# Feed-forward and down stages: one pool of 8 KB places, both sums of a product ahead of their low parts

## The chip, the core and the metric

The kernel runs on one core of one Trainium2 chip. The metric is the time of one execution on the device in microseconds (us). Five engines work side by side: TensorE (PE in the profile; its weight loads are PEld), VectorE (DVE), ScalarE (ACT), GpSimd (POOL) and SyncE (SP), whose queue issues all the DMAs that matter here.

## What is computed

One decoder block on 512 tokens of 1024 channels, in float32. Only its last step, the SwiGLU feed-forward, is touched:

```python
D_FF = 2816
h2 = rmsnorm(x, g_ffn[l])
ff = (jax.nn.silu(h2 @ w_gate[l]) * (h2 @ w_up[l])) @ w_down[l]
x = x + ff
```

## The kernel before

**Arithmetic.** Each float32 operand is split into a high part (a cast to fp32r, on ScalarE) and a low part (operand minus high part, on VectorE). A product is three matmuls: high by high, low by high, high by low. `part` (L938) makes both parts of a block of weights, 128 x 1024; `split_x` (L878) those of the tokens' side.

**Gate and up, six groups.** `GROUPS` (L915) cuts the 2816 hidden channels into five groups of 512 and one of 256. In a group the gate and up weights form a 2 by 2 block matrix B11, B12, B21, B22, each block in two halves v = 0, 1. Seven products of blocks and of sums of blocks take the place of eight. `gu` (L953) issues one product: 24 matmuls of 512 columns, the first 12 with the parts of half 0, the last 12 with those of half 1. In a group after the first, the order on TensorE is: y with B21, four transposes each of two chunks (`put_h`, L1018, the group before turned for the down product), x with B11 (two more chunks are turned in its middle), z with S1, x with S2, x with S3, z with S4, x with A22. The weights of S1, S2, S3 and A22 are sums of two blocks, made in place by VectorE (`sum_of`, L949). S3 adds to the same PSUM banks as S2, and between them `keep` (L1031, copy at L1033) saves the banks with ScalarE: S3 can't write a bank before its copy is done.

**Places.** Parts rotate over three places (`ring_parts`, L930), so the cast of a part waits until TensorE is done with the part three before it. Two of the three are separate tiles for high and low part. The blocks' halves are separate tiles of 4 KB, loaded by `load_group` (L918) when the former content of each is no longer read.

**Down.** Channels 1024 to 2815 of the hidden side are multiplied one chunk of 128 at a time: `prepare(k)` (L967) loads a chunk of `w_down` and makes the parts of it and of the turned hidden chunk, and `whole` (L1105) runs 24 matmuls into eight banks. Fourteen chunks, k = 8 to 21. Between them `p_sums` (L989) makes the sums that the last stage needs.

**Last stage.** The first 1024 hidden channels use seven products again: `factors` (L1144) loads 1 MB of `w_dh` for a group of two output chunks, makes three blocks' parts (`ah`, `al`), two sums T1, T3 (`t13`, parts `ch0`, `cl0`) and T2, T4 (`t24`, parts `ch1`, `cl1`). Its pool `wd` is opened at L1125, after `wq` is released at L1124, in the same memory, so its tiles wait until all that lay there is no longer read. The order of TensorE is pinned in the order of the code; on the other engines and in SP's queue a scheduler sets it, apart from VectorE's work in the groups, which `queue` pins.

Of the kernel before, what the change touches and what calls it, by code (L numbers as in the profile page):

```python
# [14 lines left out]
ALU = mybir.AluOpType  # L15
# [38 lines left out]
def block_kernel(ctx: ExitStack, tc, x, xT, c_early, c_tab, c_late, w_qf, w_tok, w_vg, w_a, w_y, w_o, w_gu, w_gl, w_dn, w_dh, out):  # L54
# [860 lines left out]
    GROUPS = [512] * 5 + [256]  # L915
    ring, fq = [0], None

    def load_group(g, which):  # L918
        w = GROUPS[g]
        for b in which:  # L920
            if b == B21 and g % 2:
                halves_ = fq.tile([P, 2, 1024], F32, name="b21", tag="b21")
                halves_ = [halves_[:, v, :] for v in range(2)]
            else:
                halves_ = [wq.tile([P, 1024], F32, name=f"b{b}{v}", tag=f"b{b}{v}") for v in range(2)]
            for v in range(2):
                nc.sync.dma_start(out=halves_[v][:, :2 * w], in_=w_gu[g, b, v] if w == 512 else w_gl[b, v])
            raws[g][b] = [f[:, :2 * w] for f in halves_]
# [20 lines left out]
    def sum_of(g, b, c, v):  # L949
        queue(tt(out=raws[g][b][v], in0=raws[g][b][v], in1=raws[g][c][v], op=ALU.add))  # L950
# [15 lines left out]

    def prepare(k):  # L967
        n = k - HALF
        raw = wq.tile([P, 1024], F32, name="raw", tag=("b00", "b01", "b30", "b31")[n % 4])
        nc.sync.dma_start(out=raw, in_=w_dn[n])  # L970
        h, l = ring_parts()
        cast = nc.scalar.copy(out=h, in_=raw)
        if n > 0:
            after(cast, prepare.last)
        tt(out=l, in0=raw, in1=f32(h), op=ALU.subtract)
        if n % 4 == 0:
            hl = xp.tile([P, 2, S], F32R, name="hl", tag="s4")
        elif n % 4 == 3:
            hl = fq.tile([P, 2, S], F32R, name="hl", tag="b21")
        else:  # L980
            hl = wq.tile([P, 2, S], F32R, name="hl", tag=f"b2{n % 4 - 1}")
# [4 lines left out]
        tt(out=pl, in0=pf[:, k, :], in1=f32(ph), op=ALU.subtract)  # L986
        parts_of[k] = (h, l, ph, pl)

    def p_sums(j):  # L989

        fx = wq.tile([P, 4, HT], F32, name="fx", tag="b1%d" % (j % 2))
        a11, a21, a12, a22 = (pf[:, 2 * j + m2, s2 * HT:s2 * HT + HT] for m2 in range(2) for s2 in range(2))
        tt(out=fx[:, 0, :], in0=a21, in1=a22, op=ALU.subtract)
# [32 lines left out]
    for g, w in enumerate(GROUPS):  # L1026
# [17 lines left out]
        else:  # L1044
# [14 lines left out]
        parts = [part(sum_of(g, B11, B22, v)) for v in range(2)]  # L1059
        gu(x_, parts, S2, False, w)  # L1060
        keep(1, x_)
        if g == 0:
# [1 line left out]
        for tp in range(2):  # L1064
            queue(tt(out=us[tp][:, 0, :], in0=y_[tp][:, :w], in1=us[tp][:, 0, :], op=ALU.add))  # L1065
            act(out=us[tp][:, 0, :], in_=us[tp][:, 0, :], func=AF.Silu, scale=rstd2[:, tp:tp + 1])
        parts = [part(sum_of(g, B12, B22, v)) for v in range(2)]
        if g + 1 < len(GROUPS):
            load_group(g + 1, (B12,))
        gu(x_, parts, S3, False, w)  # L1070
# [2 lines left out]
        if g + 1 < len(GROUPS):  # L1073
            load_group(g + 1, (B22,))
        gu(z_, parts, S4, False, w)
        parts = [part(sum_of(g, B11, B21, v)) for v in range(2)]
        if g + 1 < len(GROUPS):
            load_group(g + 1, (B11,))
        for tp in range(2):
# [50 lines left out]
    def wtile(tag):  # L1130

        n, dt, *other = WT[tag]
        i = seen.get(tag, 0)
        seen[tag] = i + 1
        if other and i % 2:
            return fq.tile([P, n, 512], dt, name=tag, tag=other[0])
        return wd.tile([P, n, 512], dt, name=tag, tag=tag)

    def split_to(src, tags):
        h, l = wtile(tags[0]), wtile(tags[1])  # L1140
        split_to.last = nc.scalar.copy(out=h, in_=src), tt(out=l, in0=src, in1=f32(h), op=ALU.subtract)
        return h, l

    def factors(src, behind=None):  # L1144

        raw, t13, t24 = wtile("raw"), wtile("t13"), wtile("t24")
        nc.sync.dma_start(out=raw, in_=src)
# [3 lines left out]
        factors.cast, c0 = split_to.last[0], split_to(t13, ("ch0", "cl0"))  # L1151
# [5 lines left out]
        c1 = split_to(t24, ("ch1", "cl1"))  # L1157
# [79 lines left out]
    pinned[0] = False  # L1237
    fp.release()
    fq.release()
    wd.release()  # L1240
    xp.release()
    ps.release()
    drp.release()
# [104 lines left out]
```

## Time and profile before

| | us |
|---|---|
| median of 3 runs (729.04 to 730.38) | 730.36 |
| the profiled execution itself | 730.06 |
| its span, first to last instruction | 728.3 |
| TensorE busy (97%) | 707.4 |
| TensorE weight loads (81%) | 587.7 |
| VectorE busy (71%) | 520.0 |
| ScalarE busy (51%) | 373.0 |

In the slices of the page TensorE is busy nine tenths or more nearly everywhere; the exception that stands out is the third slice from the end, with 5 tenths and a granted clock of 7 tenths, and that is where the last stage begins. The mean granted clock of TensorE is 0.990. The groups of 512 take some 41.6 us each and stand between 385 and 570 us, the narrow group ends near 595 us, the down stage near 673 us.

### The profile page before, as it was taken

The numbers are of one execution on the slowest core, as the hardware profiler recorded it, in microseconds if no ns is written. First come the engines' busy times: TensorE is split into PE (matmuls) and PEld (weight loads), VectorE is DVE, ScalarE is ACT, GpSimd is POOL, SyncE is SP. The second block draws the span as 40 slices with busy tenths as digits, with TensorE's granted clock in tenths as the row PEclk, the third lists the DMA queues.
The fourth block names the chain that finished last, engine by engine and source line by source line (L and its number), as shares of the span: only waits on it lengthen the run. The fifth ranks groups of instructions, "written<-read, shape, count | busy, mean of one in ns | idle before, by whom it ended". The sixth has DMA issues, their size and how long they took to land.

```text
span 728.3 us, 9535 instructions
## 1 busy us (share of the span) xinstructions
PE 707.4 (97%) x3599; PEld 587.7 (81%) x3599; DVE 520.0 (71%) x845; ACT 373.0 (51%) x570; POOL 72.2 (10%) x90
## 2 busy tenths in 40 slices
PE   9999999999999999999998999999999989999598
PEld 6888988888877778888886878778787978888598
DVE  6798587754877757569787878687777789334584
ACT  6677363234765583236555564655555575321251
POOL 0005940202222110002210000000000000000000
PEclk9999999999999999999999999999999999999799
DMA  8900312323433212268105124060602045210412
GB/s 284 408 6 30 118 58 89 94 85 117 126 102 93 81 50 97 89 200 317 42 17 180 52 82 151 26 206 0 198 6 59 28 156 189 90 30 1 147 64 78
DMA packets 24141, 77.29 MB, mean 106 GB/s; under 512 B 2840, under 2 KB 3480, under 8 KB 23584
## 3 DMA queue, kind: packets, MB, share of 16 engines
q1 hardware_dynamic: 23952, 76.67, 32.0%
q8 instruction: 28, 0.46, 0.3%
q14 instruction: 17, 0.14, 0.1%
q10 hardware_dynamic: 144, 0.02, 0.0%
HBM read 73.52 MB, written 2.11 MB: 104 GB/s over the span
## 4 chain that ended last, share of the span: by engine, by line
PE 80%; DVE 9%; ACT 6%; issue 3%; DMA 2%; POOL 1%; ACTq 0%; SPq 0%; DVEq 0%; POOLq 0%
PE acc L72 57%; PE sc L72 15%; PE tp L72 5%; PE tp L75 3%; ACT ph L941 3%; DVE b L950 2%; DVE pl L942 2%; DVE us L1065 1%; ACT hl L941 1%; DMA raw<-in_w_dh_dram 1%; ACT us L1033 1%; DMA raw<-in_w_tok_dram 0%; POOL cb L680 0%; DMA cb<-cd 0%; DVE tq L667 0%
## 5 line engine op out<-in xcount | busy, mean ns | idle before, releaser
L154 ACT CAST wh<-raw 128x1024 fp32r<-128x1024 f32 (+1 forms) x44 | 46.1, 1049 | 84.8 <-PE acc L72 80.7
L942 DVE TENSOR_TENSOR pl<-b,ph 128x1024 fp32r<-128x1024 f32 (+1 forms) x56 | 63.3, 1138 | 36.2 <-ACT ph L941 36.2
L72 PE MATMUL acc<-ph,xfh 128*128 128x512 f32 (+1 forms) x196 | 74.3, 379 | 2.3 <-ACT us L1033 1.3
L72 PE MATMUL acc<-pl,xfh 128*128 128x512 f32 (+1 forms) x196 | 73.7, 376 | 1.1 <-DVE pl L942 0.9
L941 ACT CAST ph<-b 128x1024 fp32r<-128x1024 f32 (+1 forms) x56 | 54.8, 983 | 38.1 <-DVE b L950 27.8
L72 PE MATMUL acc<-ph,xfl 128*128 128x512 f32 (+1 forms) x196 | 72.9, 372 | 0.0
L155 DVE TENSOR_TENSOR wl<-raw,wh 128x1024 fp32r<-128x1024 f32 (+1 forms) x44 | 56.9, 1296 | 17.3 <-ACT wh L154 17.2
L72 PE MATMUL acc<-hl,xfh 128*128 128x512 f32 (+1 forms) x184 | 59.7, 384 | 3.1 <-ACT hl L941 2.3
L950 DVE TENSOR_TENSOR b<-b,b 128x1024 f32<-128x1024 f32 (+1 forms) x48 | 54.2, 1130 | 0.1
L72 PE MATMUL acc<-xh,wh 128*128 128x512 f32 x128 | 53.2, 416 | 0.0
L72 PE MATMUL acc<-wh,xh 128*128 128x512 f32 (+2 forms) x144 | 50.4, 350 | 0.0
L72 PE MATMUL acc<-xh,wl 128*128 128x512 f32 x128 | 50.1, 392 | 0.0
L72 PE MATMUL acc<-xl,wh 128*128 128x512 f32 x128 | 50.0, 391 | 0.0
L72 PE MATMUL acc<-wh,xl 128*128 128x512 f32 (+2 forms) x144 | 49.4, 343 | 0.0
L72 PE MATMUL acc<-wl,xh 128*128 128x512 f32 (+2 forms) x144 | 49.3, 342 | 0.0
L72 PEld LDWEIGHTS acc<-ph,xfh 128*128 128x128 f32 x196 | 36.9, 188 | 10.4 <-ACT us L1033 3.2
L72 PEld LDWEIGHTS acc<-pl,xfh 128*128 128x128 f32 x196 | 36.9, 188 | 10.0 <-DVE pl L942 3.7
L72 PEld LDWEIGHTS acc<-hl,xfh 128*128 128x128 f32 x184 | 34.2, 192 | 12.3 <-DVE hl L942 2.8
L942 DVE TENSOR_TENSOR hl<-b,hl 128x1024 fp32r<-128x1024 f32 (+1 forms) x28 | 31.6, 1128 | 16.5 <-ACT hl L941 16.5
L72 PEld LDWEIGHTS acc<-ph,xfl 128*128 128x128 f32 x196 | 36.9, 188 | 6.1
L941 ACT CAST hl<-b 128x1024 fp32r<-128x1024 f32 (+1 forms) x28 | 27.3, 976 | 20.8 <-DVE b L950 9.8
L72 PE MATMUL acc<-hl,xfl 128*128 128x512 f32 (+1 forms) x92 | 34.6, 376 | 0.0
(329 smaller groups left out, 1762.7 us busy)
## 6 DMA issues: line engine op xcount, KB each, us to landing
b<-in_w_gu_dram SPq DMA_DIRECT2D x40, 512.0 KB, 4.8
raw<-in_w_a_dram SPq DMA_DIRECT2D x16, 512.0 KB, 3.6
raw<-in_w_dn_dram SPq DMA_DIRECT2D x14, 512.0 KB, 3.9
blk<-in_w_vg_dram SPq DMA_DIRECT2D x8, 512.0 KB, 10.1
raw<-in_w_tok_dram SPq DMA_DIRECT2D x8, 512.0 KB, 3.5
raw<-in_w_y_dram SPq DMA_DIRECT2D x8, 512.0 KB, 3.6
raw<-in_w_o_dram SPq DMA_DIRECT2D x8, 512.0 KB, 3.6
raw<-in_w_dh_dram SPq DMA_DIRECT2D x4, 1024.0 KB, 4.8
```

What stands on the lines that cost most here:

```text
L72: in_order(nc.tensor.matmul(o, **kw))
L75: in_order(nc.tensor.transpose(out=o, in_=src, identity=ident))
L154: split_raw.last = (nc.scalar.copy(out=h[:, :width], in_=raw[:, :width]), tt(out=l[:, :width], in0=raw[:, :width], in1=f32(h)[:, :width], ...
L155: tt(out=l[:, :width], in0=raw[:, :width], in1=f32(h)[:, :width], op=ALU.subtract))
L941: nc.scalar.copy(out=h, in_=raw)
L942: low = tt(out=l, in0=raw, in1=f32(h), op=ALU.subtract)
L950: queue(tt(out=raws[g][b][v], in0=raws[g][b][v], in1=raws[g][c][v], op=ALU.add))
L1033: nc.scalar.copy(out=us[tp][:, slot, :], in_=os[tp][:, :w])
L1065: queue(tt(out=us[tp][:, 0, :], in0=y_[tp][:, :w], in1=us[tp][:, 0, :], op=ALU.add))
```

## The change

Blocks, parts and the last stage's tiles become tiles of 8 KB that hold a pair: both halves of a block (tags `b0` to `b3`, and `b2f` for B21 of odd groups), high and low part of one ring place (`r0`, `r1`, `r2`), two raw chunks of `w_down`. The pool `wd` is gone: the last stage takes places of `wq` and `fq` by name. A place is free again when both of its halves are no longer read. In the groups, `sums_in_parts` emits both sums of a product and then the two parts. The first two chunks of `w_down` take the place of B21, which is not used by the last group, in place of that of B12. The first step of `p_sums` is ordered behind the low part of the chunk just prepared. The number and size of matmuls, casts, subtractions and DMAs stay as they were.

```diff
-            if b == B21 and g % 2:
-                halves_ = fq.tile([P, 2, 1024], F32, name="b21", tag="b21")
-                halves_ = [halves_[:, v, :] for v in range(2)]
-            else:
-                halves_ = [wq.tile([P, 1024], F32, name=f"b{b}{v}", tag=f"b{b}{v}") for v in range(2)]
+            block = pair_tile(fq if b == B21 and g % 2 else wq, F32, f"b{b}", "b2f" if b == B21 and g % 2 else f"b{b}")
+            raws[g][b] = [block[:, v, :2 * w] for v in range(2)]
...
-        if i < 2:
-            return [wq.tile([P, 1024], F32R, name=n, tag=f"{n}{i}") for n in ("ph", "pl")]
-        hl = fq.tile([P, 2, 1024], F32R, name="hl", tag="hl")
+        hl = pair_tile(fq if i == 2 else wq, F32R, "ps", f"r{i}")
         return [hl[:, v, :] for v in range(2)]
...
+    def sums_in_parts(g, b, c):
+        return [part(f) for f in [sum_of(g, b, c, v) for v in range(2)]]
...
-            parts = [part(sum_of(g, B11, B12, v)) for v in range(2)]
+            parts = sums_in_parts(g, B11, B12)
...
-        raw = wq.tile([P, 1024], F32, name="raw", tag=("b00", "b01", "b30", "b31")[n % 4])
+        if n % 2 == 0:
+            prepare.raw = pair_tile(wq, F32, "raw", "b2" if n == 0 else ("b3", "b0")[n // 2 % 2])
+        raw = prepare.raw[:, n % 2, :]
...
-        tt(out=fx[:, 0, :], in0=a21, in1=a22, op=ALU.subtract)
+        after(tt(out=fx[:, 0, :], in0=a21, in1=a22, op=ALU.subtract), prepare.low)
...
-    wq.release()
-    wd = tc.alloc_tile_pool(name="wd", bufs=1, side="right")
-    WT = {"raw": (4, F32, "us0"), "ah": (3, F32R, "b21"), "al": (3, F32R, "hl"), "t13": (2, F32), "t24": (2, F32),
-          "ch0": (2, F32R), "cl0": (2, F32R), "ch1": (2, F32R), "cl1": (2, F32R)}
+    WT = {"raw": (4, F32, (fq, "us0"), (wq, "b3")), "ah": (3, F32R, (wq, "b1"), (fq, "b2f")), "al": (3, F32R, (fq, "r2"), (wq, "r1")), "t": (4, F32, (wq, "b0")),
+          "c0": (4, F32R, (wq, "r0")), "c1": (4, F32R, (wq, "b2"))}
```

What moves is shown by the order of instructions. First VectorE, in the second group, from the end of the S2 product's preparation to the parts of S4. L950 (L947 after) is a sum of two blocks; L942 (L939 after) is a low part, written to `pl` or `hl` (`ps` after); L1065 adds y to the saved x. Before:

```order
L1065 TENSOR_TENSOR us1_3841<-sc_3847,us1_3841 128x512
L950 TENSOR_TENSOR b00_3716<-b00_3716,b30_3753 128x1024
L942 TENSOR_TENSOR pl_4006<-b00_3716,ph_4005 128x1024
L950 TENSOR_TENSOR b01_3717<-b01_3717,b31_3754 128x1024
L942 TENSOR_TENSOR hl_4010<-b01_3717,hl_4010 128x1024
L942 TENSOR_TENSOR pl_4044<-b30_3753,ph_4043 128x1024
```

and after, in the same place:

```order
L1065 TENSOR_TENSOR us1_3822<-sc_3828,us1_3822 128x512
L947 TENSOR_TENSOR b0_3705<-b0_3705,b3_3740 128x1024 x2
L939 TENSOR_TENSOR ps_3983<-b0_3705,ps_3983 128x1024
L939 TENSOR_TENSOR ps_3986<-b0_3705,ps_3986 128x1024
L939 TENSOR_TENSOR ps_4018<-b3_3740,ps_4018 128x1024
```

Both sums now stand ahead of the two low parts of S3; the same happens in S1, S2 and A22 of each group. Second ScalarE at the same place: L941 (L938 after) is the cast that makes a high part, the L1033 copies of `acc_3842` and `acc_3843` (`acc_3823`, `acc_3824` after) save the banks of x between S2 and S3. Before:

```order
L1066 ACTIVATE us1_3841<-us1_3841,rstd1_86 128x512
L941 CAST ph_4005<-b00_3716 128x1024
L1033 COPY us0_3840<-acc_3842 128x512
L941 CAST ph_4043<-b30_3753 128x1024
L1033 COPY us1_3841<-acc_3843 128x512
L941 CAST hl_4010<-b01_3717 128x1024
```

and after:

```order
L1066 ACTIVATE us1_3822<-us1_3822,rstd1_86 128x512
L938 CAST ps_3983<-b0_3705 128x1024
L938 CAST ps_3986<-b0_3705 128x1024
L1033 COPY us0_3821<-acc_3823 128x512
L1033 COPY us1_3822<-acc_3824 128x512
L938 CAST ps_4018<-b3_3740 128x1024
```

The second cast of S3 now stands ahead of both copies, and no cast stands between the copies. Third SP's queue around the last group and the start of the down stage: `b1` is B11 of the narrow group (`b10`, `b11` before), `w_dn` are the down chunks, `w_dh` the last stage's weights. Before:

```order
L927 DMA b11_4979<-in_w_gl_dram 128x512
L970 DMA raw_5293<-in_w_dn_dram 128x1024
L970 DMA raw_5344<-in_w_dn_dram 128x1024
...
L970 DMA raw_5539<-in_w_dn_dram 128x1024
L1147 DMA raw_5859<-in_w_dh_dram 128x2048
...
L970 DMA raw_5794<-in_w_dn_dram 128x1024
L1147 DMA raw_5840<-in_w_dh_dram 128x2048
```

and after:

```order
L972 DMA raw_5216<-in_w_dn_dram 128x1024 x2
L927 DMA b1_4911<-in_w_gl_dram 128x512 x2
L972 DMA raw_5303<-in_w_dn_dram 128x1024 x2
L972 DMA raw_5378<-in_w_dn_dram 128x1024 x2
L1150 DMA raw_5739<-in_w_dh_dram 128x2048
...
L972 DMA raw_5667<-in_w_dn_dram 128x1024 x2
L1150 DMA raw_5755<-in_w_dh_dram 128x2048
```

Before, the load that stood early in the queue, `raw_5859`, was that of the last stage's second group, and the first group's, `raw_5840`, stood behind all of `w_dn`. After, the early one, `raw_5739`, is the first group's. Also, VectorE makes the low parts of that group, `al_5743`, `c1_5752` and `c0_5747`, ahead of the evacuation of the second down bank; before, its sums and the low parts of its sums stood behind all eight evacuations (L1111).

More of the change, by code (lines that the diff above doesn't have):

```diff
@@ L916, in block_kernel, with pair_tile @@
     ring, fq = [0], None
+    def pair_tile(pool, dt, name, tag):
+        return pool.tile([P, 2, 1024], dt, name=name, tag=tag)
     def load_group(g, which):
@@ L985, in prepare @@
             after(prepare.last, cast)
-        tt(out=pl, in0=pf[:, k, :], in1=f32(ph), op=ALU.subtract)
+        prepare.low = tt(out=pl, in0=pf[:, k, :], in1=f32(ph), op=ALU.subtract)
         parts_of[k] = (h, l, ph, pl)
     def p_sums(j):
-        fx = wq.tile([P, 4, HT], F32, name="fx", tag="b1%d" % (j % 2))
+        fx = wq.tile([P, 4, HT], F32, name="fx", tag="b1")
         a11, a21, a12, a22 = (pf[:, 2 * j + m2, s2 * HT:s2 * HT + HT] for m2 in range(2) for s2 in range(2))
-        tt(out=fx[:, 0, :], in0=a21, in1=a22, op=ALU.subtract)
+        after(tt(out=fx[:, 0, :], in0=a21, in1=a22, op=ALU.subtract), prepare.low)
         tt(out=fx[:, 1, :], in0=fx[:, 0, :], in1=a11, op=ALU.subtract)
@@ L1058, in block_kernel @@
                 mm(pb[:, t:t + 1], lhsT=sqs[:, t * P:(t + 1) * P], rhs=ones[:, 0:1], start=True, stop=True)
-        parts = [part(sum_of(g, B11, B22, v)) for v in range(2)]
+        parts = sums_in_parts(g, B11, B22)
         gu(x_, parts, S2, False, w)
@@ L1066, in block_kernel @@
             act(out=us[tp][:, 0, :], in_=us[tp][:, 0, :], func=AF.Silu, scale=rstd2[:, tp:tp + 1])
-        parts = [part(sum_of(g, B12, B22, v)) for v in range(2)]
+        parts = sums_in_parts(g, B12, B22)
         if g + 1 < len(GROUPS):
@@ L1075, in block_kernel @@
         gu(z_, parts, S4, False, w)
-        parts = [part(sum_of(g, B11, B21, v)) for v in range(2)]
+        parts = sums_in_parts(g, B11, B21)
         if g + 1 < len(GROUPS):
@@ L1123, in block_kernel, with wtile @@
         whole(k, range(NK))
-    wq.release()
-    wd = tc.alloc_tile_pool(name="wd", bufs=1, side="right")
-    WT = {"raw": (4, F32, "us0"), "ah": (3, F32R, "b21"), "al": (3, F32R, "hl"), "t13": (2, F32), "t24": (2, F32),
-          "ch0": (2, F32R), "cl0": (2, F32R), "ch1": (2, F32R), "cl1": (2, F32R)}
+    WT = {"raw": (4, F32, (fq, "us0"), (wq, "b3")), "ah": (3, F32R, (wq, "b1"), (fq, "b2f")), "al": (3, F32R, (fq, "r2"), (wq, "r1")), "t": (4, F32, (wq, "b0")),
+          "c0": (4, F32R, (wq, "r0")), "c1": (4, F32R, (wq, "b2"))}
     seen = {}
[L1130 to L1137, printed above, removed]
-    def split_to(src, tags):
-        h, l = wtile(tags[0]), wtile(tags[1])
+    def wtile(name):
+        n, dt, *places = WT[name]
+        i = seen.get(name, 0)
+        seen[name] = i + 1
+        pool, tag = places[i % len(places)]
+        return pool.tile([P, n, 512], dt, name=name, tag=tag)
+    def split_to(src, tags):
+        if len(tags) == 1:
+            hl = wtile(tags[0])
+            h, l = hl[:, 0:2, :], hl[:, 2:4, :]
+        else:
+            h, l = wtile(tags[0]), wtile(tags[1])
         split_to.last = nc.scalar.copy(out=h, in_=src), tt(out=l, in0=src, in1=f32(h), op=ALU.subtract)
@@ L1144, in factors @@
     def factors(src, behind=None):
-        raw, t13, t24 = wtile("raw"), wtile("t13"), wtile("t24")
+        raw, t = wtile("raw"), wtile("t")
+        t13, t24 = t[:, 0:2, :], t[:, 2:4, :]
         nc.sync.dma_start(out=raw, in_=src)
@@ L1150, in factors @@
         tt(out=t13, in0=raw[:, 1:4:2, :], in1=raw[:, 0:1, :].broadcast_to([P, 2, 512]), op=ALU.add)
-        factors.cast, c0 = split_to.last[0], split_to(t13, ("ch0", "cl0"))
+        factors.cast, c0 = split_to.last[0], split_to(t13, ("c0",))
         factors.casts = factors.cast, split_to.last[0]
@@ L1239, in block_kernel @@
     fq.release()
-    wd.release()
+    wq.release()
     xp.release()
```

15 lines of the change are left out of this document (6 added, 9 removed).

## Prediction

> **What bounds the kernel now.** I read the page first: engines, chain, costly groups.
>
> ```profile
> PE 707.4 (97%) x3599; PEld 587.7 (81%) x3599; DVE 520.0 (71%) x845; ACT 373.0 (51%) x570; POOL 72.2 (10%) x90
> PE 80%; DVE 9%; ACT 6%; issue 3%; DMA 2%; POOL 1%; ACTq 0%; SPq 0%; DVEq 0%; POOLq 0%
> L942 DVE TENSOR_TENSOR pl<-b,ph 128x1024 fp32r<-128x1024 f32 (+1 forms) x56 | 63.3, 1138 | 36.2 <-ACT ph L941 36.2
> L950 DVE TENSOR_TENSOR b<-b,b 128x1024 f32<-128x1024 f32 (+1 forms) x48 | 54.2, 1130 | 0.1
> ```
>
> TensorE sets the time, and 15% of the chain runs over VectorE and ScalarE. The two groups of VectorE say why: every sum (1.13 us) is followed by a wait for a cast of the same data before the low part (1.14 us) can run; these waits come to 36.2 us on `pl` alone. Next I read who makes TensorE wait from 380 us on, the stages of the change.
>
> ```profile
> PE sc L72 <- ACT ah L1141: 6.5, 1, 6.5
> PE acc L72 <- ACT us L1033: 1.7, 7, 0.3
> ```
>
> The longest is one wait for the last stage's first cast. The other row, like those not shown, looks small, but a stretch by stretch view (columns: stretch, length, then busy time and count of PE, PEld, DVE, ACT, POOL, the granted clock, DMA) shows that they are not:
>
> ```profile
> 469.20:510.80 41.60, 40.76 (x185) 32.95 (x184) 32.56 (x33) 23.93 (x32) 0.00 (x0) 1.00 0.31 101
> 584.10:597.00 12.90, 10.71 (x78) 9.45 (x77) 10.27 (x21) 9.25 (x18) 0.00 (x0) 1.00 0.48 164
> 597.00:673.00 76.00, 76.00 (x340) 62.98 (x340) 42.67 (x65) 27.76 (x42) 0.00 (x0) 1.00 0.27 84
> 673.00:689.00 16.00, 7.95 (x42) 7.02 (x41) 10.42 (x11) 4.21 (x6) 0.00 (x0) 0.68 0.39 131
> ```
>
> In the down stage, which never stalls, weight loads fill 62.98 / 76.00 = 82.9%. In a group of 512 they fill 79.2% of 41.60 us; at 82.9% the same loads would take 39.8 us. So a group loses 1.8 us, where the busy time of PE shows only 0.84 us idle. The Trainium skill (Perfetto Trace Analysis, Identifying the Most-Contended Engine) says that matmul busy time is a poor measure of TensorE's headroom and weight-load busy time a good one; by matmul busy time my group term below would be 0.6 us a group instead of 1.35, and the sum 3.0 us smaller. These rows side with the page.
>
> **Part 1: the last stage's weights load early.** TensorE around 673 us, the DMA issue, and a stretch of the chain of waits in the last stage:
>
> ```profile
> 673.23 0.39 PE L72 MATMUL tp<-hl,pl 128*128 128x512 f32 x1
> 680.08 0.58 PE L72 MATMUL sc<-xfh,ah 128*128 128x256 f32 x1 [6.47 <-ACT ah L1141]
> 688.69 0.28 PE L72 MATMUL acc<-xfh,ah 128*128 128x256 f32 x1
> 673.65 15.50 SPq L1147 DMA_DIRECT2D raw<-in_w_dh_dram  x3
> 691.74 1.44 PE acc L72 x12
> ```
>
> The load is issued at 673.65, 0.4 us after the last matmul of the down stage began, because its pool lies in `wq`'s memory. From 673.23 to 688.69, TensorE does one down matmul and the first three products, 36 matmuls. Unhindered, a matmul of 256 columns takes 1.44 / 12 = 0.12 us, so this is 0.23 + 36 x 0.12 = 4.55 us of work in 15.46 us: 10.9 us lost, part of it waiting and part at a clock of 0.68 (the last row of stretches). After the change, `raw` sits in `us0`, free once the last group is turned (near 600 us), and the load is issued there. `ah`, `al` and T2's parts take places that fall free two or more chunks before the end (24 matmuls of 0.227 us, the pitch of part 2, are 5.44 us a chunk). The closest is `c0` for T1 and T3: `r0`, last used by the 13th chunk, free one chunk before the end; low part and cast of 1024 columns cost 1.14 us (above) and 1.05 us (the cast in part 2), and T1 is needed 1.44 us after the end. That leaves over 4 us. VectorE does these ahead of seven evacuations, which then end some 3 us after the last down matmul; the first banks that the last stage reuses are evacuated first. The second group's `ah` waits for the 14th chunk's place and is needed 10.1 us later (seven products), a cover four times its cost. I take 10.8 us; bounds 8.5 (a bubble of 2.3 us, `c0` after all at the end) and 10.9.
>
> **Part 2: sums ahead of low parts, groups 2 to 5.** The end of S2 and S3 in one of them, on PE, ACT and DVE:
>
> ```profile
> 510.81 0.39 PE L72 MATMUL acc<-pl,xfh 128*128 128x512 f32 x1
> 511.47 0.50 PE L72 MATMUL acc<-hl,xfh 128*128 128x512 f32 x1 [0.27 <-ACT us L1033]
> 512.25 0.49 PE L72 MATMUL acc<-hl,xfh 128*128 128x512 f32 x1
> 512.90 0.50 PE L72 MATMUL acc<-hl,xfh 128*128 128x512 f32 x1 [0.16 <-ACT us L1033]
> 515.30 0.39 PE L72 MATMUL acc<-ph,xfl 128*128 128x512 f32 x1
> 515.74 0.50 PE L72 MATMUL acc<-pl,xfh 128*128 128x512 f32 x1
> 510.85 0.57 ACT L1033 COPY us<-acc 128x512 f32<-128x512 f32 x1
> 511.32 1.05 ACT L941 CAST ph<-b 128x1024 fp32r<-128x1024 f32 x1
> 510.97 1.23 DVE L942 TENSOR_TENSOR hl<-b,hl 128x1024 fp32r<-128x1024 f32 x1 [1.18 <-ACT hl L941]
> 514.45 2.36 DVE L942 TENSOR_TENSOR pl<-b,ph 128x1024 fp32r<-128x1024 f32 x2 [1.12 <-ACT ph L941]
> 609.70 2.72 PE acc L72 x12
> ```
>
> Full pitch is 2.72 / 12 = 0.227 us (last row, the chain in the down stage). Matmuls start late by 0.43 us at 511.47 (the copy of x's first bank), 0.21 at 512.25 (the low part that ends at 512.2), 0.42 at 512.90 (the second copy, behind a cast) and 0.21 at 515.74 (the low part that ends near 515.6); each restart costs about 0.1 more. That is 1.6 us, near the 1.8 above. Emitting both sums first lets the second cast run during the first low part: of two waits of 1.12 to 1.18 us in a pair, about both go, some 2 us of VectorE a pair, in three pairs before S3. Then both low parts of S3 are done before TensorE wants them, and the two late starts on low parts vanish. No cast stands between the copies, so the 0.42 goes. The copy itself can't be hidden: x's first bank ends three matmuls before S2 does, so part of the 0.43 stays. With 0.15 and one restart of 0.1 left, the gain is 1.35 us a group, 5.4 for four. What hides the second sum in front of the first low part is the cast (about 1 us against 1.13): the low part comes at most 0.1 us later. Bounds: 0 (the casts wait for their ring place, not for the sum) and 6.4.
>
> **Part 3: the first group.** S3 there starts very late:
>
> ```profile
> 383.28 0.39 PE L72 MATMUL acc<-pl,xfh 128*128 128x512 f32 x1
> 385.98 0.79 PE L72 MATMUL acc<-hl,xfh 128*128 128x512 f32 x1 [2.31 <-ACT hl L941]
> 383.33 1.05 ACT L1033 COPY us<-acc 128x512 f32<-128x512 f32 x2
> 384.27 0.73 ACT L1066 ACTIVATE us<-us,rstd 128x512 f32<-128x512 f32 x1
> 384.89 1.04 ACT L941 CAST hl<-b 128x1024 fp32r<-128x1024 f32 x1
> 387.00:390.00 3.00, 2.96 (x9) 2.25 (x9) 1.89 (x3) 1.05 (x1) 0.00 (x0) 0.60 0.54 162
> ```
>
> The cast of S3's first part stands behind both copies and a silu on ScalarE. After the change both silus stand ahead of the copies, and VectorE is 2 us early, so their inputs are there. The cast then follows the copies, at about 384.2 instead of 384.89: 0.7 us gained. The rest of the wait stays, and I keep the low clock after it (0.60 in the last row) as it is. Bounds 0 and 2.0 (the wait gets short enough for the clock to hold). The Trainium skill (TensorE: Matmul & The Clock Gate, What's actually happening) has the clock fall after about one idle window of 3.4 us; by that a wait of 1.6 us would keep it and the sum would be 1.3 us larger. But here 2.31 us sufficed for 0.60, so I don't count on it.
>
> **Part 4: the narrow group and the first down chunk.**
>
> ```profile
> 584.06 0.28 PE L72 MATMUL acc<-hl,xfh 128*128 128x256 f32 x1
> 585.32 0.39 PE L72 MATMUL acc<-ph,xfh 128*128 128x256 f32 x1 [0.98 <-ACT ph L941]
> 595.49 0.63 PE L72 MATMUL sc<-hl,ph 128*128 128x512 f32 x2
> 596.74 0.50 PE L72 MATMUL sc<-hl,pl 128*128 128x512 f32 x1 [0.61 <-DVE pl L975]
> 591.73 0.42 DVE L993 TENSOR_TENSOR fx<-pf 128x256 f32<-128x256 f32 x1
> ```
>
> From 584.06 to 595.49 there are 73 matmuls of 256 columns, 8.76 us, in 11.43: 2.7 lost, since latencies stay while products are half as long. The next row adds 1.25 - 0.45 = 0.8 for the low part of the first down chunk, which VectorE reached late, also because three `p_sums` steps (0.33 us each, from 591.73) had slipped in ahead; they are now ordered behind `prepare.low`. The chunk's load leaves earlier and was not what ended last. Of 3.5 us I leave 0.2 for the copy of x: 3.3. Bounds 1.5 (the 1.14 before S3 and 0.7 elsewhere stay) and 3.5.
>
> **Costed at nothing.** Pair tiles for ring places: a cast now waits for the last of three matmuls, 0.23 us later, covered by the two parts in between (2.72 us each). Raw pairs of `w_down`: the load of chunk n waits for chunk n-3's neighbour too, with over 10 us in hand at 5.44 us a chunk. SP's queue: `w_dh` waits for `us0` ahead of the seventh chunk's load, which is needed three chunks later.
>
> **Sum.** 10.8 + 5.4 + 0.7 + 3.3 = 20.2 us. The profiled execution took 730.06, so 709.9; it lies 0.3 below the median of 730.36, within the runs' spread.
>
> **Rivals.** (a) *The groups keep their stalls*: casts wait for ring places, so the reordered sums buy nothing in groups 2 to 5. For it: casts already wait for PE in places. Against: by my working each place falls free over 2.7 us before the part is needed. 20.2 - 5.4: 715.3. (b) *The last stage still starts with a bubble* because one of its places is freed by the last chunk: 2.3 us waiting and some at a low clock, 3 us: 712.9. (c) *The change does not do what it says*: `w_dh` still arrives at the end since a place or the queue holds it; only parts 2 to 4 remain, 9.4 us: 720.7. The queue order speaks against it. (d) *Slower*: pairs delay the load of the next group's B11, since its first half can leave only when both halves are read.
>
> ```profile
> 482.24 1.23 DVE L942 TENSOR_TENSOR hl<-b,hl 128x1024 fp32r<-128x1024 f32 x1 [1.17 <-ACT hl L941]
> 493.70 0.48 PE L72 MATMUL acc<-hl,xfh 128*128 128x512 f32 x1
> b<-in_w_gu_dram SPq DMA_DIRECT2D x40, 512.0 KB, 4.8
> ```
>
> The second half is read at 483.4 already before the change, and TensorE wants the first part at 493.70; less a cast and its neighbours in the queue, the load has 9 us and takes 4.8. It hurts from 9 us on, and the kernel is slower only if the five loads lose over 4 us each (13 us a load): then 731 or more.
>
> Chances: forecast 0.73, (a) 0.12, (b) 0.08, (c) 0.05, (d) 0.02. The range runs from 707.0 (all four terms at their upper bounds, 22.8 us, and 0.3 for the spread of runs) to 717.0, which takes in (a) and (b) and a part of the lower bounds; (c) and (d) stay out. A measurement of this kernel can tell about 0.2% (1.5 us) from no change: faster 0.96, same 0.02, slower 0.02.
>
> **What would show it.** Right: `w_dh` issued near 600 us; no PE wait on `ah` and a clock of 1.0 after the down stage; S2's last matmuls 40.2 us apart from group to group instead of 41.6; VectorE's waits for casts mostly gone; the down stage starting 9 us earlier. Wrong: `ACT us` waits over 0.4 us in the groups, waits on `ps` low parts, or a new PE wait on `c0`, B loads or raw chunks.

## The result, and the profile after

The changed kernel takes 709.27 us (median of 4 runs, 707.73 to 709.5), beside 729.82 us (729.04 to 730.38) for the kernel before. The ratio is 0.9715, with a 95% interval of 0.9697 to 0.9733. The profiled execution took 709.5 us with a span of 707.7 us, 20.6 us below the 728.3 us of before.

The page of the changed kernel, its engines, its chain and the two groups that make the parts (L939 the low part, L938 the cast):

```profile
PE 699.0 (99%) x3599; PEld 584.6 (83%) x3599; DVE 521.5 (74%) x845; ACT 375.2 (53%) x570; POOL 72.5 (10%) x90
PE 44%; ACT 0%; DVE 0%; issue 0%; ACTq 0%
L939 DVE TENSOR_TENSOR ps<-b,ps 128x1024 fp32r<-128x1024 f32 (+1 forms) x84 | 94.8, 1136 | 40.7 <-ACT ps L938 39.9
L938 ACT CAST ps<-b 128x1024 fp32r<-128x1024 f32 (+1 forms) x84 | 82.2, 981 | 52.7 <-PE acc L72 37.0
```

The work is the same (3599 matmuls, DVE 521.5 us busy), and TensorE is at 99%. The chain can be followed back over only 44% of the span here, nearly all of it on TensorE, so its shares can't be set beside those of before. VectorE still waits 39.9 us for casts; before, the group `pl` waited 36.2 us, and the group `hl` 16.5:

```profile
L942 DVE TENSOR_TENSOR hl<-b,hl 128x1024 fp32r<-128x1024 f32 (+1 forms) x28 | 31.6, 1128 | 16.5 <-ACT hl L941 16.5
```

The last row of the changed kernel's page above says why these waits do little harm now: the casts in turn wait 37.0 us for TensorE (`PE acc`), that is, for a place that is still being read. VectorE now waits because it is early. TensorE's only wait for a low part of a block that the trace lists is one of 0.53 us, in the first group.

The same stretches as before, on the changed kernel: one group of 512 from S2's last matmul to the next group's, the down stage, and the 16 us behind it:

```profile
466.73:506.97 40.24, 40.24 (x185) 33.07 (x184) 32.93 (x34) 24.21 (x32) 0.00 (x0) 1.00 0.30 105
588.00:664.00 76.00, 76.00 (x342) 63.04 (x341) 47.53 (x72) 30.52 (x45) 0.00 (x0) 1.00 0.28 97
664.00:680.00 16.00, 16.00 (x135) 15.97 (x135) 13.70 (x16) 7.69 (x12) 0.00 (x0) 1.00 0.24 84
```

Weight loads fill 33.07 / 40.24 = 82.2% of a group now, against 79.2% before and 82.9% in the down stage. The last row has 135 matmuls at a clock of 1.00 in the time in which before had 42 at 0.68.

**The last stage.** SP's queue and TensorE at the seam between the down stage and the last stage:

```profile
591.69 0.33 SPq L1150 DMA_DIRECT2D raw<-in_w_dh_dram  x1
662.34 1.52 PE L72 MATMUL tp<-hl,ps 128*128 128x512 f32 x6
663.70 0.28 PE L72 MATMUL sc<-xfh,ah 128*128 128x256 f32 x1
668.01 0.28 PE L72 MATMUL acc<-xfh,ah 128*128 128x256 f32 x1
```

The load is issued at 591.69 and the first product follows the last down matmul (662.34 + 5 x 0.227 = 663.47) with no wait. From that last down matmul to the fourth product it takes 4.54 us, where before took 688.69 - 673.23 = 15.46.

**A group.** The end of S2 and the start of S3 in the fourth group, on TensorE, then VectorE, then ScalarE:

```profile
506.97 0.89 PE L72 MATMUL acc<-ps,xfh 128*128 128x512 f32 x2
507.70 0.40 PE L72 MATMUL acc<-ps,xfl 128*128 128x512 f32 x1
...
502.71 2.35 DVE L947 TENSOR_TENSOR b<-b,b 128x1024 f32<-128x1024 f32 x2
505.10 2.38 DVE L939 TENSOR_TENSOR ps<-b,ps 128x1024 fp32r<-128x1024 f32 x2
...
504.01 2.21 ACT L938 CAST ps<-b 128x1024 fp32r<-128x1024 f32 x2 [0.23 <-DVE b L947]
506.72 1.26 ACT L1033 COPY us<-acc 128x512 f32<-128x512 f32 x2 [0.49 <-PE acc L72]
```

Two sums, two low parts, each pair back to back; both casts ahead of both copies. Both low parts of S3 end at 507.48, before TensorE is through S3's first matmuls, and only one late start is left: the first row holds S2's last matmul and S3's first, and the second starts 507.70 - 506.97 - 2 x 0.227 = 0.28 us late.

**The first group, and the narrow one.** TensorE, then two stretches of the first group:

```profile
383.93 0.39 PE L72 MATMUL acc<-ps,xfh 128*128 128x512 f32 x1
385.94 0.50 PE L72 MATMUL acc<-ps,xfh 128*128 128x512 f32 x1 [1.62 <-ACT ps L938]
387.20 0.73 PE L72 MATMUL acc<-ps,xfh 128*128 128x512 f32 x2 [0.53 <-DVE ps L939]
...
577.22 0.77 PE L72 MATMUL acc<-ps,xfh 128*128 128x256 f32 x2
586.34 1.80 PE L72 MATMUL sc<-hl,ps 128*128 128x512 f32 x6
587.97 0.85 PE L72 MATMUL acc<-hl,ps 128*128 128x512 f32 x3
```

```profile
386.00:388.00 2.00, 1.47 (x5) 0.91 (x6) 2.00 (x2) 1.78 (x2) 0.00 (x0) 1.00 0.00 0
388.00:390.00 2.00, 2.00 (x10) 1.67 (x9) 1.42 (x2) 0.20 (x1) 0.00 (x0) 1.00 0.36 51
```

S3 of the first group still waits, 1.62 us for its cast and 0.53 us for a low part, and the clock stays at 1.00 behind it. From S2's last matmul of the narrow group (577.22) to the third bank of the first down chunk (587.97) it takes 10.75 us; before took 597.76 - 584.06 = 13.70 (the same matmul starts at 597.76 there). Two late starts are in the 10.75 us: S3's first matmul of the narrow group comes 0.37 us late with its restart, released by the first copy, and the third matmul of the first down chunk 0.27 us late with its restart, released by that chunk's low part (L977).

Where the 20.6 us came from, by these marks (the distances of S2's last matmuls are in the table under the experiments):

| stretch | before | after | gain | predicted |
|---|---|---|---|---|
| part 1, last down matmul to the fourth product | 15.46 | 4.54 | 10.9 | 10.8 |
| part 2, groups 2 to 5, S2's end to S2's end | 156.48 | 150.67 | 5.8 | 5.4 |
| part 3, first group | 44.30 | 42.62 | 1.7 | 0.7 |
| part 4, narrow group and first down chunk | 13.70 | 10.75 | 2.95 | 3.3 |
| before the first group's S2 ends | 383.28 | 383.93 | -0.65 | 0 |

The last row lies in stages that the change doesn't touch. The experiments' executions differ there by up to 2.1 us (the norm's first matmul of the first group starts between 376.0 and 378.1 us), and two executions of one kernel by up to 1.6 us; spans of single executions are compared below only from there on.

### The profile page after: what moved, and what is told of

The parts are those of the page before. It is cut to its first block, busy times and chain, and to the rows that moved or that the text cites. A ratio compares the mean times of both kernels' runs of the same rounds, so it can differ in the third digit from the quotient of the medians.

```text
span 707.7 us, 9510 instructions
## 1 busy us (share of the span) xinstructions
PE 699.0 (99%) x3599; PEld 584.6 (83%) x3599; DVE 521.5 (74%) x845; ACT 375.2 (53%) x570; POOL 72.5 (10%) x90
## 5 line engine op out<-in xcount | busy, mean ns | idle before, releaser
L72 PE MATMUL acc<-ps,xfh 128*128 128x512 f32 (+1 forms) x576 | 170.2, 375 | 2.3 <-ACT ps L938 1.6
L72 PEld LDWEIGHTS acc<-ps,xfh 128*128 128x128 f32 x576 | 105.2, 188 | 23.9 <-ACT us L1033 2.3
L939 DVE TENSOR_TENSOR ps<-b,ps 128x1024 fp32r<-128x1024 f32 (+1 forms) x84 | 94.8, 1136 | 40.7 <-ACT ps L938 39.9
L938 ACT CAST ps<-b 128x1024 fp32r<-128x1024 f32 (+1 forms) x84 | 82.2, 981 | 52.7 <-PE acc L72 37.0
L72 PE MATMUL acc<-ps,xfl 128*128 128x512 f32 (+1 forms) x288 | 107.0, 372 | 0.0
L72 PEld LDWEIGHTS acc<-ps,xfl 128*128 128x128 f32 x288 | 54.3, 189 | 8.7
L947 DVE TENSOR_TENSOR b<-b,b 128x1024 f32<-128x1024 f32 (+1 forms) x48 | 52.3, 1130 | 0.5 <-DMA b<-in_w_gu_dram 0.5
L72 PE MATMUL acc<-hl,ps 128*128 128x512 f32 x168 | 40.4, 389 | 0.0
L72 PEld LDWEIGHTS acc<-hl,ps 128*128 128x128 f32 x168 | 31.5, 188 | 6.6
L1033 ACT COPY us<-acc 128x512 f32<-128x512 f32 (+1 forms) x48 | 26.4, 551 | 18.3 <-PE acc L72 16.6
L977 DVE TENSOR_TENSOR ps<-raw,ps 128x1024 fp32r<-128x1024 f32 x14 | 17.1, 1224 | 21.7 <-ACT ps L974 21.7
L72 PEld LDWEIGHTS acc<-wh,xh 128*128 128x128 f32 x144 | 27.2, 189 | 3.6 <-ACT wh L154 0.2
L72 PEld LDWEIGHTS acc<-wl,xh 128*128 128x128 f32 x144 | 27.2, 189 | 2.9
```

Of the source, the lines that this page charges most:

```text
L72: in_order(nc.tensor.matmul(o, **kw))
L939: low = tt(out=l, in0=raw, in1=f32(h), op=ALU.subtract)
L1033: nc.scalar.copy(out=us[tp][:, slot, :], in_=os[tp][:, :w])
```

## The experiments

My theory: the terms are separate and add up; parts 2 to 4 come from the order of sums, casts and low parts, part 1 from where the last stage's tiles lie. The rivals are named with each experiment. All times below are medians; the ratios are to the kernel before on the same chip.

### The order of the sums, undone and alone

Undone, in the changed kernel:

```diff
-        return [part(f) for f in [sum_of(g, b, c, v) for v in range(2)]]
+        return [part(sum_of(g, b, c, v)) for v in range(2)]
```

> The changed kernel (709.3 us), with each sum followed by its own part again, as before the change; pools, places and the last stage stay changed. My theory: the order of sums and casts alone makes parts 2 and 3 and most of the narrow group's share of part 4 (5.8 + 1.7 + about 1.5 of 2.95 us), so about 718 us (716.5 to 719), with S2's last matmuls 41.6 us apart again and waits of S3 for a low part or a copy. Rival: part 2 came from the pair places or from the loads, and not from the order: then the time stays within 1.5 us of 709.3 and the spacing stays near 40.2 us.

Measured: 719.22 us (717.51 to 720.19), ratio 0.9851 (0.9829 to 0.9872). The order is worth 9.9 us, a little more than the upper end that I gave. Late starts on a copy and on a low part stand in S3 of the fourth group again:

```profile
512.53 0.50 PE L72 MATMUL acc<-ps,xfh 128*128 128x512 f32 x1 [0.27 <-ACT us L1033]
516.79 0.50 PE L72 MATMUL acc<-ps,xfh 128*128 128x512 f32 x1 [0.44 <-DVE ps L939]
597.62 0.73 PE L72 MATMUL sc<-hl,ps 128*128 128x512 f32 x2 [0.61 <-DVE ps L977]
```

The last row is the wait in the first down chunk, which I had left out of the order's share: 0.61 us, as before the change.

Alone, in the kernel before, in the four places where a product's parts are made:

```diff
-            parts = [part(sum_of(g, B11, B12, v)) for v in range(2)]
+            parts = [part(f) for f in [sum_of(g, B11, B12, v) for v in range(2)]]
```

> The kernel before (729.8 us), with both sums ahead of the parts and nothing else of the change: single tiles and the last stage's own pool as before. My theory: the terms add, so this takes 5.8 (groups 2 to 5), 1.7 (first group) and about 1.5 to 2 (narrow group) from 729.8: 720 to 721 us, with S2's last matmuls 40.2 us apart. Rival one: pair places cost something that the order's gain covered up: then the spacing here is below 40.1 us and the time below 719. Rival two: single places let a cast start later than its sum, and the gain needs the pairs: then 724 us or more.

Measured: 721.83 us (721.02 to 722.39), ratio 0.9888 (0.9873 to 0.9903): 8.2 us gained, some 1 us less than expected. Distances of S2's last matmuls, in us:

| | group 1 to 2 | 2 to 3 | 3 to 4 | 4 to 5 | 5 to 6 |
|---|---|---|---|---|---|
| before | 44.30 | 41.63 | 41.60 | 41.56 | 31.69 |
| sums in turn, rest changed | 44.10 | 42.35 | 41.63 | 41.56 | 31.68 |
| sums first, rest as before | 42.62 | 40.95 | 40.24 | 41.24 | 30.71 |
| sums first and ring places as pairs | 42.62 | 40.24 | 40.19 | 40.24 | 29.95 |
| changed kernel | 42.62 | 40.18 | 40.24 | 40.24 | 30.01 |

With the order alone three of five distances fall short of the changed kernel's, together by 2.5 us. The pairs without the order (second line) gain nothing: its five distances add up to 201.32 us, those of before to 200.78, those of the order alone to 195.76. ScalarE and TensorE of this kernel at the end of S2 in the fourth group show why:

```profile
506.14 0.59 ACT L1033 COPY us<-acc 128x512 f32<-128x512 f32 x1 [0.72 <-PE acc L72]
506.92 1.05 ACT L941 CAST ph<-b 128x1024 fp32r<-128x1024 f32 x1 [0.19 <-PE acc L72]
507.87 0.58 ACT L1033 COPY us<-acc 128x512 f32<-128x512 f32 x1
...
508.50 0.50 PE L72 MATMUL acc<-hl,xfh 128*128 128x512 f32 x1 [0.74 <-ACT us L1033]
```

A cast of 1.05 us stands between the two copies, and S3 waits 0.74 us for the second copy. That is neither of my first explanations: single places don't delay the cast (rival two), they let it in front of the copy. So one part of the change that I had costed at nothing, the pairs, was left to test.

> The kernel before (729.8 us) with both sums ahead of the parts, and the three ring places as pairs of high and low part; blocks, down chunks and the last stage as before. With the new order alone S2's last matmuls stood 40.2 to 41.2 us apart, since in some groups ScalarE had a cast between the two copies of x; with pairs no cast stands there. Theory: the ring pairs are what is worth the missing 2.5 us in the groups, through that order: about 719.4 us (718.6 to 720), spacing 40.2 us in every group. Rival: the missing part came from the pairs of blocks or of down chunks: then 721.5 us or more and a spacing of over 41 us in some group.

The edit, to the kernel of the order alone:

```diff
-            return [wq.tile([P, 1024], F32R, name=n, tag=f"{n}{i}") for n in ("ph", "pl")]
+            ps = wq.tile([P, 2, 1024], F32R, name="ps", tag=f"r{i}")
+            return [ps[:, v, :] for v in range(2)]
```

Measured: 720.79 us (719.21 to 721.06), ratio 0.9872 (0.9852 to 0.9892). The table's fourth line is the changed kernel's, within 0.06 us in every group, and no cast stands between the copies in any group of 512 or the narrow one. So the places as pairs, by way of ScalarE's order, are worth 2.5 us in the groups on top of the sums' order, and neither the blocks nor the down chunks are needed for it. The median falls by only 1.0 us, 1.4 above my figure and outside the range that I gave, with overlapping intervals; this kernel's last stage took 15.98 us between the marks of part 1, 0.5 us more than the order alone (15.44), and what else differs isn't settled by four runs each.

### The last stage's places, undone alone

The edit gives back the pool `wd`, opened after `wq` is released, with before's tiles (`t13`, `t24`, `ch0` to `cl1`) and factors:

```diff
-    WT = {"raw": (4, F32, (fq, "us0"), (wq, "b3")), "ah": (3, F32R, (wq, "b1"), (fq, "b2f")), "al": (3, F32R, (fq, "r2"), (wq, "r1")), "t": (4, F32, (wq, "b0")),
-          "c0": (4, F32R, (wq, "r0")), "c1": (4, F32R, (wq, "b2"))}
+    wq.release()
+    wd = tc.alloc_tile_pool(name="wd", bufs=1, side="right")
+    WT = {"raw": (4, F32, "us0"), "ah": (3, F32R, "b2f"), "al": (3, F32R, "r2"), "t13": (2, F32), "t24": (2, F32),
+          "ch0": (2, F32R), "cl0": (2, F32R), "ch1": (2, F32R), "cl1": (2, F32R)}
...
```

> The changed kernel (709.3 us), with the last stage's tiles in a pool of their own again, opened after the places of the feed-forward are given back, as before the change. My theory: exactly part 1 is lost, 10.9 us: 720.2 us (719.5 to 721), with the first w_dh load issued at the end of the down stage, a TensorE wait of about 6.5 us for the first cast and a granted clock near 0.68 after it. Rival: part of the 10.9 us came from the order of VectorE's work (low parts ahead of evacuations) or from the clock of the stages before; then it loses less than 9 us.

Measured: 721.49 us (720.25 to 721.88), ratio 0.9881 (0.9865 to 0.9898): 12.2 us lost, 1.3 more than expected. SP and TensorE of this kernel, and the clock in 4 us stretches:

```profile
664.11 0.33 SPq L1147 DMA_DIRECT2D raw<-in_w_dh_dram  x1
671.55 0.58 PE L72 MATMUL sc<-xfh,ah 128*128 128x256 f32 x1 [7.47 <-ACT ah L1141]
```

```profile
668.00:672.00 4.00, 0.45 (x2) 0.45 (x2) 1.87 (x3) 1.97 (x2) 0.00 (x0) 0.67 0.10 41
672.00:676.00 4.00, 2.58 (x12) 2.28 (x12) 4.00 (x5) 0.45 (x1) 0.00 (x0) 0.50 0.00 0
676.00:680.00 4.00, 4.00 (x22) 4.00 (x21) 2.86 (x4) 1.69 (x3) 0.00 (x0) 0.55 0.74 262
```

The wait is 7.47 us, not 6.47. The load itself took 5.9 us (issued 664.11, first read near 670.0) instead of 4.9, and TensorE then ran at half clock until almost 680. Between the marks of part 1 the five executions that have the stall measure 15.46 and 15.40 (before, two executions), 15.44 (the order alone), 15.98 (with ring pairs) and 16.84 us (here), against 4.54 without it: part 1 is worth 10.9 to 12.3 us. The rival falls, since the loss is larger than forecast and not smaller.

### Two edits that I had costed

The first two chunks of `w_down` back in the place of B12:

```diff
-            prepare.raw = pair_tile(wq, F32, "raw", "b2" if n == 0 else ("b3", "b0")[n // 2 % 2])
+            prepare.raw = pair_tile(wq, F32, "raw", ("b0", "b3")[n // 2 % 2])
```

> The changed kernel (709.3 us), with the first two chunks of w_down in the place of B12 and so on in turn, as before the change, instead of in that of B21. My theory: the first chunk's load then leaves later but still lands well ahead of its use, since the load was not what ended last in the first down chunk: 709.3, within 0.5 us. Rival: the earlier load is worth part of the 2.95 us that part 4 gained: 710.5 us or more, with a PE wait on the parts of the first chunk.

Measured: 709.29 us (707.24 to 709.67), ratio 0.9708 (0.9686 to 0.9729). As expected: the load was not what ended last.

The first step of `p_sums` free again:

```diff
-        after(tt(out=fx[:, 0, :], in0=a21, in1=a22, op=ALU.subtract), prepare.low)
+        tt(out=fx[:, 0, :], in0=a21, in1=a22, op=ALU.subtract)
```

> The changed kernel (709.3 us) with the first step of p_sums free again, not ordered behind the low part of the chunk just prepared. My theory: three steps of 0.33 us slip ahead of the low part of the first down chunk, and TensorE waits 0.3 to 0.7 us for it: 709.6 to 710. Rival: the wait for that low part came from the order of sums and casts in the narrow group (the kernel with sums in turn had it back although the step was pinned), so freeing it costs nothing: 709.3, within 0.2 us, and no wait on that part.

Measured: 708.90 us (708.0 to 709.58), ratio 0.9713 (0.9694 to 0.9732), and the trace lists no wait of TensorE on a part of the down chunks; the late start of 0.27 us in the first of them, on its low part, is there with and without the pin. The rival is right: the pin buys nothing. The wait of 0.61 us in the first down chunk came from the order of sums in the narrow group, as its return in the first experiment had hinted, where the step was pinned.

### What is left in the groups

Two waits stand in the changed kernel's first group, and 0.28 us in each group after it. For the first, S3's sums and parts are made in the first group ahead of the norm and the silus:

```diff
         if g == 0:
+            parts = sums_in_parts(g, B12, B22)
             turn_of[0] = rsqrt(rstd2, pb[:, 0:NT], 1.0 / D, [P, NT], "n1", behind=turn_of[0])
...
-        parts = sums_in_parts(g, B12, B22)
+        if g > 0:
+            parts = sums_in_parts(g, B12, B22)
```

> The changed kernel (709.3 us) with the sums and parts of the first group's S3 ahead of the norm's work and the silus there. My theory: in the first group the cast of S3 waits for ScalarE's place in the order alone; with it ahead, the waits of 1.62 us for the cast and 0.53 for the low part go, and only the copy's 0.27 stays: 707.2 us (706.8 to 707.7). Rival: the silus and the norm then come late, and x's products or z's evacuation wait for them: no gain, 709 us or more.

Measured: 706.41 us (705.55 to 707.40), ratio 0.9680 (0.9660 to 0.9700). The gain is 2.9 us in the medians, and the time lies 0.4 us below the range that I gave; from the norm's first matmul to the first down chunk it is 208.56 - 206.19 = 2.4 us, and TensorE waits for no part in the groups any more. The theory holds; the rest of the 2.9 us isn't settled by four runs each. Next, S2 by bank, so that the first bank of x ends earlier:

```diff
-        gu(x_, parts, S2, False, w)
+        gu(x_, parts, S2, False, w, by_bank=True)
```

> The kernel with the first group's S3 parts ahead, and also S2's matmuls by bank, so that x's first bank ends 12 matmuls and not 3 before S2 does. Theory: the copy of the first bank is then done before S3 needs it, and the 0.27 us left in each group goes: 1.3 to 1.6 us less than the kernel without it, about 705.8. Rival: by bank, each part of half 1 is needed 12 matmuls earlier for the second half of each bank, and its cast or low part is late: 0.3 us a group or more lost, with TensorE waits for parts.

Measured: 705.72 us (704.99 to 706.80), ratio 0.9667 (0.9647 to 0.9687). The number is the one expected, but neither the gain nor the mechanism: it is 0.7 us below the kernel without the edit instead of 1.3 to 1.6, and from the norm to the first down chunk it takes 206.20 us, as without the edit, so what differs lies ahead of it. ScalarE and TensorE at the end of S2 in the third group:

```profile
462.08 0.58 ACT L1033 COPY us<-acc 128x512 f32<-128x512 f32 x1
464.52 0.59 ACT L1033 COPY us<-acc 128x512 f32<-128x512 f32 x1 [0.26 <-PE acc L72]
...
464.77 0.89 PE L72 MATMUL acc<-ps,xfh 128*128 128x512 f32 x2
465.50 0.40 PE L72 MATMUL acc<-ps,xfl 128*128 128x512 f32 x1
```

The first copy is early, as intended: it starts 2.0 us ahead of S2's last matmul (at 464.09), where it started 0.25 us ahead without the edit. But the second bank now ends with S2, its copy runs to 465.11, and S3, which takes the banks in turn every three matmuls, needs that bank after three. The second matmul of the third row, S3's fourth, starts at 465.16 behind the copy, and the one after it, in the last row, is again 0.27 us late. So S3 by bank as well:

```diff
-        gu(x_, parts, S3, False, w)
+        gu(x_, parts, S3, False, w, by_bank=True)
```

> The kernel with the first group's S3 parts ahead and S2 by bank, and now S3's matmuls by bank too. By bank in S2 alone the 0.27 us before S3 moved from S3's first matmul to its fourth, the first that writes the second bank: it waits for the second copy. Theory: with S3 by bank twelve matmuls stand between its start and the second bank, both copies are hidden, and the 0.27 us of five groups and 0.37 of the narrow one go: 1.7 us less than the 706.4 and 705.7 us of the two kernels before it, 704.0 to 704.8. Rival: S3's second part is then needed six matmuls earlier (1.36 us), and its cast or low part is late: a TensorE wait of 0.2 us or more in each group, 705.5 us or more.

Measured: 705.22 us (704.70 to 706.82), ratio 0.9662 (0.9645 to 0.9679). The time lies between the range of the theory and that of the rival, and both hold in part. The groups are 39.9 us apart, 0.3 us less, and no late start is left between S2 and S3. But in the first group and in the first down chunk low parts are late:

```profile
395.36 0.73 PE L72 MATMUL acc<-ps,xfh 128*128 128x512 f32 x2 [0.47 <-DVE ps L939]
583.05 1.20 PE L72 MATMUL sc<-hl,ps 128*128 128x512 f32 x4 [0.41 <-DVE ps L977]
```

Hence the last version, with `by_bank=0 < g < 5` in both products:

> The kernel with the first group's S3 parts ahead, and S2 and S3 by bank only in groups 2 to 5. With both by bank everywhere those groups lost their 0.27 us each (39.9 us apart instead of 40.2), but the first group lost about 1.0 us to low parts and starts, and the first down chunk 0.59 us instead of 0.27. Theory: the four groups keep their gain of 0.3 us each, and the first group and the first down chunk lose only the old 0.27: from the first group's start to the first down chunk 205.0 us (206.2 with the parts ahead alone), in all about 704.9 us, 1.2 to 1.5 us under 706.4. Rival: the losses move with the groups, and the time stays at 705.2 or above.

Measured: 704.91 us (704.48 to 705.95, 5 runs), ratio 0.9661 (0.9648 to 0.9674). From the norm to the first down chunk it takes 205.01 us, the forecast figure. The late starts between S2 and S3 are gone in groups 2 to 5; those on the copy stay in the first group and the narrow one, and the 0.27 us on the low part in the first down chunk. It is 0.6% faster than the changed kernel, and its interval lies wholly below that of the change (0.9697 to 0.9733). It overlaps those of the three versions before it, so that it beats them is not shown by the times, only by the stretch from the norm to the first down chunk, in one execution of each.

### The clock in the first group

After the first profiles a contradiction stood: with the sums in turn S3 waited 2.33 us in the first group, like before, but the clock stayed at 1.00. Both kernels were run and profiled once more.

> The kernel before, unchanged, for a second look at the first group: S3 waits 2.31 us for its cast there, and the granted clock was 0.50 to 0.66 in the 4 us after it; with the sums in turn in the changed kernel a wait of 2.33 us left it at 1.00. One theory: the wait of 2.3 us is enough and the other case was an exception: 0.50 to 0.66 again. The other: what decides is where the wait falls in a window that runs by itself, so that one and the same wait gives 1.00 in one execution and 0.5 in another: a clock of 1.00 here would show it, 0.5 would leave it open.

> The changed kernel with sums and parts in turn once more, for a second look at its first group: a wait of 2.33 us, after which the granted clock stayed 1.00. One theory, that the length decides: 1.00 again. The other, that the place in a window that runs by itself decides: it may be near 0.5 this time; 1.00 would leave it open.

S3's first matmul and the clock behind it, first the second execution of before:

```profile
385.09 0.50 PE L72 MATMUL acc<-hl,xfh 128*128 128x512 f32 x1 [2.31 <-ACT hl L941]
386.35 0.73 PE L72 MATMUL acc<-hl,xfh 128*128 128x512 f32 x2 [0.53 <-DVE hl L942]
389.83 0.50 PE L72 MATMUL acc<-pl,xfh 128*128 128x512 f32 x1 [0.46 <-DVE pl L942]
386.00:390.00 4.00, 3.19 (x13) 2.33 (x14) 2.88 (x4) 2.06 (x2) 0.00 (x0) 1.00 0.39 131
```

then the sums in turn, the first execution:

```profile
386.52 0.50 PE L72 MATMUL acc<-ps,xfh 128*128 128x512 f32 x1 [2.33 <-ACT ps L938]
386.00:390.00 4.00, 2.96 (x12) 2.11 (x13) 2.39 (x3) 2.46 (x3) 0.00 (x0) 1.00 0.00 0
```

and the second:

```profile
384.87 0.50 PE L72 MATMUL acc<-ps,xfh 128*128 128x512 f32 x1 [2.31 <-ACT ps L938]
386.00:390.00 4.00, 3.87 (x10) 3.09 (x11) 2.89 (x4) 1.04 (x1) 0.00 (x0) 0.57 0.00 0
```

Both kernels changed sides: before went from 0.50 and 0.66 (386 to 388 and 388 to 390 us of its first execution) to 1.00, the sums in turn from 1.00 to 0.57, with the same wait. So the length of this wait doesn't decide. That agrees with the Trainium skill (TensorE: Matmul & The Clock Gate, What's actually happening), by which the clock follows a window of activity that runs by itself; the runs show the chance in it, not the window's length. The idle window of about 3.4 us that the prediction quotes from there is longer than the wait of 2.31 us that took the clock down in two executions here; the measurement decides, and why the shorter wait suffices stays open. The second execution of before (728.91 us, and 719.41 for the sums in turn, one run each) shows what the low clock had cost: its first group takes 426.46 - 382.39 = 44.07 us instead of 44.30, only 0.2 us, since further waits for low parts (0.53 and 0.46 us, in place at 1.00) disappear behind matmuls that run slower.

## Why the prediction was right, and where not

The forecast of 709.9 us was right in the whole and in the order of its terms. That it came within 0.7 us is in part luck: in the two profiled executions the four terms gained 21.4 us, 1.2 more than forecast, and 0.65 of that was lost again by chance in the stages ahead of the change.

**Part 1** (10.8 against 10.9): right by its steps, the early issue, no wait on `ah`, the clock at 1.00, `c0` in time. What I took for a fixed size depends on how long the load and the low clock last: 10.9 to 12.3 us in the runs that have the stall.

**Part 2** (5.4 against 5.8): the size was right, the credit wrong in part. I ascribed it to "Emitting both sums first" that no cast stands between the copies; the runs show that in three of the five distances this needs the ring places as pairs, the edit that I had costed at nothing, having thought of the cast's place only. Of the 200.78 - 193.29 = 7.5 us that the table's five distances lost in all, the order alone brings 5.0, and the pairs, on top of it, 2.5. The reason in the scheduler, that a pair comes free later in its reckoning and so the cast loses its turn to the copy, is argued and was not tested.

**Part 3** (0.7 against 1.7): the step that failed is "The rest of the wait stays, and I keep the low clock after it". The cast came 0.69 us earlier (a wait of 1.62 instead of 2.31), as worked out. The other 1.0 us I left standing. In the trace of before it shows as slow matmuls: from S3's first matmul to its thirteenth it takes 390.63 - 385.98 = 4.65 us there and 3.66 us after, at a clock of 1.00. But most of it is not the clock's. What I didn't see is a late low part of S3's second half, 0.46 us of wait, which sets TensorE back by 0.74 us with the restart. At the low clock of the trace of before it was covered by slow matmuls, so no row showed it; at a clock of 1.00 it stands there (389.83 in the second execution of before), and the new order removes it, just as in part 2 (the order alone, in the table's third line, gives the whole 1.7 us). So 1.7 is 0.7 for the cast, 0.74 for this low part and 0.2 for the low clock, and that last term is chance, since the same wait gives either clock.

**Part 4** (3.3 against 2.95): the 0.2 us that I left for the copy were 0.37 us in the narrow group, and I left nothing for the low part of the first down chunk, which still costs 0.27. The steps of `p_sums` were named as a cause of the late low part; they weren't, since freeing them changes nothing.

**Costed at nothing**: raw pairs, SP's queue and the new place for the first down chunks held. Rival (a)'s mechanism is there, since casts wait 37.0 us for places, but without the stalls. One sign that I had listed for a right forecast, "VectorE's waits for casts mostly gone", did not come: 39.9 of 52.7 us are left. Rivals (b) and (c) left no trace: no wait on `c0`, and the load at 591.69. Of (d) there is little: VectorE waits 0.5 us in all for a block's load, TensorE for none.

## What to carry to other kernels

When an engine alternates between making an operand and waiting for another engine's half of it, emit the makers together, and then look at what the new order lets into the other engine's queue: here one cast between two copies, in three groups, took 2.5 us of the 7.5 that the distances lost. A pool that opens late in another's memory made the tiles in it wait for the last reader of that memory (the load at 664.11 instead of 591.69); places by name wait only for their own. And a stall at a low clock hides others: count what would be late at full clock before a term is set to what one execution shows.

## What was not expected of the hardware

- One wait of 2.31 to 2.33 us of TensorE left its clock at 1.00 in two executions and took it to 0.50 to 0.66 for about 4 us in two others, two kernels showing both.
- The stall in front of the last stage, with a first wait of 6.4 to 7.5 us, cost 10.9 to 12.3 us, the difference lying in the load (4.9 to 5.9 us for 1 MB, from issue to the first read) and in how long TensorE ran at half its rate behind the wait (5.3 to 8.0 us at 0.213 us a matmul of 256 columns instead of 0.12).
